# Stationary weight tiles stored in seven turns of layout in a two-block forward pass on one core

## The chip, the cores and the metric

The kernel runs on one core of a Trainium2 chip. The metric is the device time of one execution in microseconds (us), the median of the runs shown. The core has TensorE (PE in the profile, with its weight loads shown apart as PEld), VectorE (DVE), ScalarE (ACT), GpSimd (POOL) and the DMA queues, of which SP issues the weight loads.

## The reference, cut to what matters

Two blocks follow one another on 512 tokens of width 1024, float32 throughout. The first adds 16 meta tokens, and computes

```
n  = rms(h);  z = n @ w_in                     # q, k, v, glu, two gates: 7168 columns
u  = silu(layernorm(conv31(glu_a * sigmoid(glu_b)))) @ w_conv_out
m  = sigmoid(g_att) * diff_attention(q, k, v) + sigmoid(g_conv) * u
h  = h + m @ w_out
gate, val = split(conv3(rms(h) @ w_up))        # 2 x 2816 columns
h  = h + (silu(gate) * val) @ w_down
x  = rms(h)
```

The second block does this twice (two layers): `proj = rms(x) @ w_in` with 8192 columns, a gated three-tap convolution on one half, rotary retention with eight heads on the other half, then `x = x + rms(mix @ w_out)`.

Nearly all arithmetic is in these products with weights. Each is done in three TensorE passes: every operand is split into a high part of a short type (fp32r) and the remainder, and the product is high x high + low x high + high x low.

## The kernel before, in words

The activations lie with the model dimension on the partitions: eight tiles of 128 partitions by 512 to 528 token columns, once as the high part (`xh`) and once as the low part (`xl`), in one buffer `xhome`. A weight tile is 128 partitions by 1024 float32 columns (768 for the third part of w_down): eight 128x128 blocks beside one another, one for each 128 rows of the product's inner dimension.

`order` (line 75 on) lists the 300 weight tiles in the order in which they are used. `prep` (line 125) takes the next: SP's queue loads it into `wraw` (line 134, two buffers), ACT rounds it into `wh` (line 137), DVE subtracts to get `wl` (line 138). `getw` (line 141) keeps LOOK + 1 = 4 tiles prepared. 24 of the tiles hold the weights of v; in these products the weights are the moving operand (lines 473 and 806). The other 276 are stationary: `proj` (line 150) runs, for one output tile of n token columns in PSUM, three passes over the eight blocks, that is 24 matmuls at line 156 (18 for the short w_down tile), each with a 128x128 block of `wh` or `wl` as the stationary operand (its own weight load) and n columns of `xh` or `xl` as the moving one.

The column counts n follow the stage: 264 and 264 for the glu tiles (16 tiles, names gv and gg) and for k; 258 and 256 for q, the two gates (ga, gc), w_conv_out (yc) and w_out (wo); 258 and 258 for w_up (up, 44 tiles); 512 for w_down (dn), for the second block's projections (rq, rk, rz, cc, cx, cb, cz) and its w_out (w), except for the last tile of w_down, q and k of the first head of a layer and the last two outputs of a layer, which run as 256 and 256. By these loops line 156 issues 9522 matmuls: 5892 of 256 to 264 columns and 3630 of 512.

The program is written with a planner that orders each engine's instructions from its own estimate of durations; pools give the buffers, and a tile's writer waits for the readers of the buffer's last content. The 31-tap convolution of the first block runs on DVE (line 399) during the attention, at a low priority.

Of the kernel before, what the change touches and what calls it, by code (L numbers as in the profile page):

```python
# [14 lines left out]
ALU = mybir.AluOpType  # L15
# [3 lines left out]
P = 128  # L19
# [21 lines left out]
KB = 1  # L41
PSF = (4, 3, 1)
GC_EARLY = 5

PAR = {}
_off = 0
# [16 lines left out]
def kernel(ctx, tc, hT, par, pos, decay, w1, w2, out):  # L63
    nc = tc.nc
    V, S, PE = nc.vector, nc.scalar, nc.tensor
# [7 lines left out]
    def fv(ap):  # L73
        return ap.bitcast(F32)


    order = []

    def w1_tiles(name, idx):
        order.append((w1[name], idx))  # L80

    for cc in range(NK):
        w1_tiles("w_in", 24 + cc)
        w1_tiles("w_in", 32 + cc)
    for h in range(HEADS):
        if h % 2 == 0:
            order.append((w1["w_v"], h))
            order.append((w1["w_v"], h + 1))
        w1_tiles("w_in", h)
        w1_tiles("w_in", 8 + h)  # L90
        if h < HEADS - 1:
            w1_tiles("w_in", 40 + h)
        if h < GC_EARLY:
            w1_tiles("w_in", 48 + h)
    w1_tiles("w_in", 40 + HEADS - 1)
    for n in range(GC_EARLY, NK):
        w1_tiles("w_in", 48 + n)
# [6 lines left out]
        w1_tiles("w_up", NF + j)  # L104
    for n in range(NK):
        for g in range(3):
            order.append((w1["w_down"], (n, g, slice(None), slice(0, (8, 8, 6)[g] * P))))
    for l in range(2):
        for h in range(HEADS):
            if h % 2 == 0:  # L110
                order.append((w2["w_v"], (l, h)))
                order.append((w2["w_v"], (l, h + 1)))
            for base in (32, 40, 56):
                order.append((w2["w_in"], (l, base + h)))
        for cc in range(NK):
            for base in (8, 16, 0, 24):
                order.append((w2["w_in"], (l, base + cc)))
        for n in range(NK):
            for g in (1, 0):
                order.append((w2["w_out"], (l, n, g)))  # L120

    ready = []
    state = {"next": 0}

    def prep():
        if state["next"] >= len(order):
            return
        src, idx = order[state["next"]]
        i = state["next"]
        state["next"] += 1  # L130
        src = src[idx]
        n = src.shape[1]
        raw = wpool.tile([P, D], F32, tag="wraw", bufs=2, name=f"wraw{i}")[:, :n]
        nc.sync.dma_start(raw, src)
        wl = wpool.tile([P, D], F32R, tag="wl", name=f"wl{i}")
        wh = wpool.tile([P, D], F32R, tag="wh", name=f"wh{i}")
        S.copy(wh[:, :n], raw)  # L137
        V.tensor_tensor(wl[:, :n], raw, fv(wh[:, :n]), ALU.subtract)  # L138
        ready.append((wh, wl))

    def getw():
        while len(ready) < LOOK + 1 and state["next"] < len(order):
            prep()
        return ready.pop(0)

    def ks(k):
        return slice(k * P, (k + 1) * P)

    def proj(ps, w, xh, xl, t0, n, nk=NK, first=True, last=True, late=0):


        wh, wl = w
        passes = ((wh, xh), (wl, xh), (wh, xl))
        steps = [(a, b, k) for r in (range(nk - late), range(nk - late, nk)) for a, b in passes for k in r]
        for i, (a, b, k) in enumerate(steps):
            PE.matmul(ps, lhsT=a[:, ks(k)], rhs=b[k][:, t0:t0 + n],  # L156
                      start=first and i == 0, stop=last and i == len(steps) - 1)

    def split(src, hi, lo):
# [22 lines left out]
    def later(steps, by=20000):  # L182

        at_ = tc.cur_priority
        tc.cur_priority = at_ + by
        steps()
        tc.cur_priority = at_


    class SumSq:  # L190


        def __init__(self, tag, slot="nacc"):
            self.acc = npool.tile([P, T1], F32, tag=slot, name=f"acc_{tag}")
            self.tag, self.seen = tag, {}
# [45 lines left out]
    def mmA(name):  # L241
        return psA.tile([P, 512], F32, tag="mm", name=name)
# [15 lines left out]
    for c0, cn in C528:  # L258
        for j in range(NK // 2):
            nc.sync.dma_start(ht2[j][:, :, c0:c0 + cn], hT[2 * j:2 * j + 2, :, c0:c0 + cn].rearrange("k p t -> p k t"))  # L260
            if c0 == 0 and j in (0, 3):
                prep()
        if c0 == 0:
            nc.sync.dma_start(pr[:, 8:], par[:, 8:])

    xu = [[hpool.tile([P, T1], F32R, tag=f"x{p}", name=f"xu{p}{k}") for k in range(NK)] for p in "hl"]
    for c0, cn in C528:
        c = slice(c0, c0 + cn)
# [109 lines left out]
    for i, (q0, qn, nkey) in enumerate(QT):  # L378
        nb = -(-nkey // P)
        t = ap1.tile([P, nb * P], F32, name=f"a{i}")  # L380
# [51 lines left out]
    def g_conv(n):  # L432
        w = getw()
        if n < 6:
            t = ap1.tile([P, TQ], F32, name=f"tgc{n}")
        else:
            t = upool.tile([P, CONV_K - 1 + T1], F32, tag="u", name=f"tgc{n}")
        for i, (c0, cn) in enumerate(C514):
            ps = mmA(f"gc{n}_{i}")[:, :cn]
            proj(ps, w, xh, xl, TQ0 + c0, cn)  # L440
            S.activation(t[:, c0:c0 + cn], ps, AF.Tanh, scale=0.5)
        tgc.append(t)

    def g_att(h):
        w = getw()
        tg = ap2.tile([P, TQ], F32, tag="tga", name=f"tga{h}")
        for i, (c0, cn) in enumerate(C514):
            ps = mmA(f"ga{h}_{i}")[:, :cn]
            proj(ps, w, xh, xl, TQ0 + c0, cn)
            S.activation(tg[:, c0:c0 + cn], ps, AF.Tanh, scale=0.5)  # L450
        return tg
# [8 lines left out]
    for h in range(HEADS):  # L460
# [3 lines left out]
        if h % 2 == 0:  # L464
            wa, wb = getw(), getw()
            for tb in range(5):
                m = P if tb < 4 else META
                ps = mmA(f"v{h}_{tb}")[:m, :256]
# [9 lines left out]
        for i, (c0, cn) in enumerate(C514):  # L478
            ps = mmA(f"q{h}_{i}")[:, :cn]
            proj(ps, w, xh, xl, TQ0 + c0, cn)  # L480
            c = slice(c0, c0 + cn)
# [11 lines left out]
        for i, (c0, cn) in enumerate(C528):  # L493
            ps = mmA(f"k{h}_{i}")[:, :cn]
            proj(ps, w, xh, xl, c0, cn)
            c = slice(c0, c0 + cn)
# [5 lines left out]
        if h < HEADS - 1:  # L502
            tg = g_att(h)
        if h < GC_EARLY:
            g_conv(h)
        if h == HEADS - 1:
            att_rstd(("kf", "kl"))
            tg = g_att(h)
            later(norm_2, N2)
            for n in range(GC_EARLY, NK):  # L510
                later(lambda: g_conv(n), GCL)
# [11 lines left out]
        for t, (q0, qn, nkey) in enumerate(QT):  # L523
# [3 lines left out]
            if t < 4:  # L527
                ps = psS.tile([P, 2, 512], F32, tag="ps", name=f"s{h}_{t}")
# [9 lines left out]
            else:  # L538
                for m in range(2):
                    ps = psS.tile([P, 1024], F32, tag="ps", name=f"s{h}_{t}_{m}")  # L540
# [23 lines left out]
            src = ptr[:, :nb * qw].rearrange("p (b q) -> p b q", b=nb)  # L564
# [3 lines left out]
        for aT, q0, qn, blocks in (  # L568
# [10 lines left out]
            ps = psO.tile([P, 512], F32, tag="tr", name=f"pss{h}_{q0}")  # L579
            if h < HEADS - 1:  # L580
                PE.matmul(ps[:, :qn], lhsT=ones, rhs=sq[:, :qn], start=True, stop=True)
                g, r = SSQ[h]
# [12 lines left out]
    for n in range(NK):  # L595
        w = getw()
        for i, (c0, cn) in enumerate(C514):
            c = slice(c0, c0 + cn)
            ps = mmA(f"yc{n}_{i}")[:, :cn]
            proj(ps, w, uh, ul, c0, cn)  # L600
            V.scalar_tensor_tensor(tgc[n][:, c], tgc[n][:, c], 1.0, ps, ALU.add, ALU.mult)
        for i, (c0, cn) in enumerate(C514):
            c = slice(c0, c0 + cn)
            pb = rs7[:, c]
            if n < NK - 1:
                pb = mmA(f"rb{n}_{i}")[:, :cn]
                g, r = SSQ[n]
# [22 lines left out]
    for n in range(NK):  # L630
# [4 lines left out]
        t = lp2.tile([P, TQ], F32, tag="hre", name=f"hre{n}")  # L635
        nc.gpsimd.dma_start(t, hT[n][:, TQ0:])
        for i, (c0, cn) in enumerate(C514):
            ps = psM.tile([P, 512], F32, tag="mm", name=f"wo{n}_{i}")[:, :cn]
# [15 lines left out]
    def mmF(name):  # L654
        return psF.tile([P, 512], F32, tag="mm", name=name)
# [6 lines left out]
    for i, (c0, cn) in enumerate(C514):  # L662
        c = slice(c0, c0 + cn)
# [36 lines left out]
    for j in range(NF):  # L700
# [5 lines left out]
        for half in range(2):  # L706
            w = getw()
            f = half * NF + j
            for c in range(2):
                ps = mmF(f"up{f}_{c}")[:, :258]  # L710
                proj(ps, w, xh, xl, c * 256, 258)
                g = fp2.tile([P, 258], F32, tag="cg", name=f"cg{f}_{c}")
                V.tensor_tensor(g, ps, rs[:, c * 256:c * 256 + 258], ALU.mult)  # L713
                t = fp2.tile([P, 256], F32, tag=f"cv{half}", bufs=3 - half, name=f"cv{f}_{c}")
# [19 lines left out]
    for n in range(NK):  # L734
        ps = mmF(f"dn{n}")
        ws = [getw() for g in range(3)]
        for c0, cn in HALF if n == NK - 1 else ((0, SEQ),):
            c = slice(c0, c0 + cn)
# [4 lines left out]
        for c0, cn in HALF:  # L743
            c = slice(c0, c0 + cn)
# [10 lines left out]
    for l in range(2):  # L755
# [16 lines left out]
        else:  # L772
            for h0, hn in HALF:
                c = slice(h0, h0 + hn)
# [19 lines left out]
        for h in range(HEADS):  # L794
# [60 lines left out]
            ps = mmF(f"rz{l}{h}")  # L855
# [5 lines left out]
            for j, i0 in enumerate((0, 128, 256, 384)):  # L861
                n = SEQ - i0
                ps = psR.tile([P, 512], F32, tag="st", name=f"st{l}{h}{j}")[:, :n]
# [34 lines left out]
        for cc in range(NK):  # L898
            def ctile(tag, n=SEQ):

                if cc == 1 and tag == "yv":
                    return npool.tile([P, T1], F32, tag="nacc2", name=f"{tag}{l}{cc}")
                if cc == 1:
                    slot = {"pp": "csr", "ct": "snr"}[tag]
                    return b2pool.tile([P, 2 + SEQ], F32, tag=slot, name=f"{tag}{l}{cc}")
                if cc == 0:
                    return npool.tile([P, T1], F32, tag="ntmp", bufs=3, name=f"{tag}{l}{cc}")
                return cp.tile([P, n], F32, tag=tag, name=f"{tag}{l}{cc}")
# [3 lines left out]
            ps = mmF(f"cc{l}{cc}")  # L912
            proj(ps, getw(), xh, xl, 0, SEQ)
            t = ctile("ct")[:, :SEQ]
            V.tensor_tensor(t, ps, rs2, ALU.mult)
            ps = mmF(f"cx{l}{cc}")
# [7 lines left out]
            ps = mmF(f"cb{l}{cc}")  # L924
# [3 lines left out]
            ps = mmF(f"cz{l}{cc}")  # L928
# [137 lines left out]
```

## Time and profile before

| | |
|---|---|
| median of 2 runs | 1887.53 us (1887.47 to 1887.59) |
| the profiled execution's own time | 1886.62 us |
| its span on the core | 1884.7 us |
| mean granted TensorE clock | 0.995 of full speed |
| PE busy, weight loads busy | 98%, 89% of the span |
| DVE, ACT, POOL busy | 70%, 44%, 4% of the span |
| moved by DMA | 177.79 MB, mean 94 GB/s |

The span is the time from the first to the last instruction of the profiled execution; 1.9 us of its time lie around it. A matmul's busy time in the profile includes its way through the array, so matmuls that follow one another overlap in the record; what one costs in a row of many is read from the distance between their starts. The chain that ended last tells which engine's work set the time in each stretch.

### The profile page before, as it was taken

The page shows a single profiled execution, that of the slowest core. Times are in us where ns is not written, and L with a number is a line of the kernel's source. Part 1 is how long each engine was busy: PE and PEld are TensorE (multiplying, and loading weights), DVE is VectorE, ACT ScalarE, POOL GpSimd, SP SyncE. Part 2 cuts the span into 40 slices and gives each one's busy share as a digit, 9 for nine tenths or more (in the row PEclk, how much of TensorE's full clock was granted, in tenths as well). Part 3 has the DMA queues.
Part 4 walks back from the last instruction along what each step waited for, and adds up shares of the span by engine and source line. Part 5 has one row for each costly group of instructions (what it writes and reads, how often), then busy time and mean ns, then how long its engine had stood idle before and what let it go on. Part 6 is the DMA issues. An engine that isn't in the chain of part 4 may idle for free.

```text
span 1884.7 us, 29258 instructions
## 1 busy us (share of the span) xinstructions
PE 1854.0 (98%) x11802; PEld 1685.0 (89%) x11802; DVE 1312.0 (70%) x2147; ACT 838.6 (44%) x1475; POOL 75.9 (4%) x123
## 2 busy tenths in 40 slices
PE   8999999989999999999999999999999999999997
PEld 7999999989999999988988888888898888888887
DVE  8999999766788777634588776554277877745424
ACT  7234455584445445433356553222255555422222
POOL 3000011000000000000000000000020000000000
PEclk9999999999999999999999999999999999999999
DMA  4332323213332222232223232232223222233231
GB/s 153 101 113 91 102 83 110 91 57 101 107 101 96 96 91 90 86 102 94 100 79 101 79 98 92 90 101 97 93 68 101 95 96 89 78 101 99 91 101 56
DMA packets 53047, 177.79 MB, mean 94 GB/s; under 512 B 6640, under 2 KB 10736, under 8 KB 52912
## 3 DMA queue, kind: packets, MB, share of 16 engines
q1 hardware_dynamic: 47696, 160.80, 25.5%
q0 software_dynamic: 5072, 15.12, 3.0%
q8 instruction: 93, 1.52, 0.3%
q14 instruction: 42, 0.34, 0.1%
q10 hardware_dynamic: 144, 0.00, 0.0%
HBM read 165.25 MB, written 2.10 MB: 89 GB/s over the span
## 4 chain that ended last, share of the span: by engine, by line
PE 94%; ACT 2%; DVE 2%; issue 1%; POOL 0%; DMA 0%; DVEq 0%; ACTq 0%; POOLq 0%
PE up L156 13%; PE w L156 9%; PE dn L156 6%; PE rz L156 5%; PE cb L156 5%; PE cc L156 5%; PE cx L156 5%; PE cz L156 5%; PE rv L806 5%; PE rq L156 5%; PE rk L156 5%; PE v L473 3%; PE k L156 3%; PE wo L156 2%; PE q L156 2%; PE ga L156 2%
## 5 line engine op out<-in xcount | busy, mean ns | idle before, releaser
L137 ACT CAST wh<-wraw 128x1024 fp32r<-128x1024 f32 (+1 forms) x300 | 313.3, 1045 | 485.3 <-PE dn L156 66.8
L138 DVE TENSOR_TENSOR wl<-wraw,wh 128x1024 fp32r<-128x1024 f32 (+1 forms) x300 | 364.2, 1215 | 187.7 <-ACT wh L137 187.0
L156 PE MATMUL up<-xhome,wh 128*128 128x258 f32 x1408 | 184.0, 282 | 0.0
L156 PEld LDWEIGHTS up<-xhome,wh 128*128 128x128 f32 x1408 | 175.1, 188 | 0.1
L399 DVE SCALAR_TENSOR_TENSOR y<-u,pr,y 128x514 f32<-128x514 f32 x240 | 170.5, 742 | 0.4 <-ACT y L397 0.2
L156 PE MATMUL up<-xhome,wl 128*128 128x258 f32 x704 | 98.8, 282 | 0.0
L156 PEld LDWEIGHTS up<-xhome,wl 128*128 128x128 f32 x704 | 90.4, 188 | 0.0
L719 DVE SCALAR_TENSOR_TENSOR cv<-cg,pr,cv 128x256 f32<-128x256 f32 x176 | 83.7, 479 | 7.9 <-ACT cv L716 6.5
L716 ACT ACTIVATE cv<-cg,pr 128x256 f32<-128x256 f32 x88 | 52.6, 598 | 63.6 <-DVE cg L713 63.6
L806 PE MATMUL rv<-wh,xhome 128*128 128x256 f32 x512 | 75.4, 286 | 0.3 <-ACT xhome L232 0.3
L156 PE MATMUL rq<-xhome,wh 128*128 128x512 f32 (+1 forms) x288 | 69.9, 372 | 1.1 <-ACT xhome L232 1.0
L806 PEld LDWEIGHTS rv<-wh,xhome 128*128 128x128 f32 x512 | 67.8, 191 | 2.0 <-ACT xhome L232 0.6
L156 PE MATMUL rk<-xhome,wh 128*128 128x512 f32 (+1 forms) x288 | 68.6, 369 | 0.0
L156 PE MATMUL w<-ml,wh 128*128 128x512 f32 (+1 forms) x320 | 66.9, 350 | 0.0
L156 PE MATMUL w<-mh,wh 128*128 128x512 f32 (+1 forms) x320 | 66.6, 350 | 0.0
L156 PE MATMUL w<-mh,wl 128*128 128x512 f32 (+1 forms) x320 | 66.2, 349 | 0.0
L156 PE MATMUL rz<-xhome,wh 128*128 128x512 f32 x256 | 66.0, 392 | 0.0
L156 PE MATMUL cx<-xhome,wh 128*128 128x512 f32 x256 | 64.0, 390 | 0.0
L156 PE MATMUL cc<-xhome,wh 128*128 128x512 f32 x256 | 63.7, 390 | 0.0
L156 PE MATMUL cb<-xhome,wh 128*128 128x512 f32 x256 | 63.7, 390 | 0.0
L889 DVE RECIPROCAL rsq<-rsq 128x512 f32<-128x512 f32 x16 | 53.6, 3350 | 14.1 <-ACT rsq L888 14.1
L156 PE MATMUL cz<-xhome,wh 128*128 128x512 f32 x256 | 63.3, 389 | 0.0
(377 smaller groups left out, 3993.7 us busy)
## 6 DMA issues: line engine op xcount, KB each, us to landing
wraw<-w_in SPq DMA_DIRECT2D x160, 512.0 KB, 3.2
wraw<-w_up SPq DMA_DIRECT2D x44, 512.0 KB, 3.2
wraw<-w_out SPq DMA_DIRECT2D x40, 512.0 KB, 3.2
wraw<-w_v SPq DMA_DIRECT2D x24, 512.0 KB, 3.2
wraw<-w_down SPq DMA_DIRECT2D x16, 512.0 KB, 3.2
qh<-qf POOLq DMA_DIRECT2D x32, 129.0 KB, 2.7
wraw<-w_conv_out SPq DMA_DIRECT2D x8, 512.0 KB, 3.2
dc<-dec POOLq DMA_DIRECT2D x16, 256.0 KB, 3.0
```

The costliest lines, as they stand in the source:

```text
L137: S.copy(wh[:, :n], raw)
L138: V.tensor_tensor(wl[:, :n], raw, fv(wh[:, :n]), ALU.subtract)
L156: PE.matmul(ps, lhsT=a[:, ks(k)], rhs=b[k][:, t0:t0 + n], start=first and i == 0, stop=last and i == len(steps) - 1)
L399: V.scalar_tensor_tensor(ys[i][:, :TQ], src, wj, ys[i][:, :TQ], ALU.mult, ALU.add)
L473: PE.matmul(ps, lhsT=x, rhs=w, start=p == 0 and k == 0, stop=p == 2 and k == NK - 1)
L716: S.activation(t, g[:, 0:256], AF.Identity, scale=pr[:, o:o + 1], bias=pc("ffn_dw_b", f))
L719: V.scalar_tensor_tensor(t, g[:, k:k + 256], pr[:, o:o + 1], t, ALU.mult, ALU.add)
L806: PE.matmul(ps, lhsT=xx, rhs=w, start=p == 0 and k == 0, stop=p == 2 and k == NK - 1)
L889: V.reciprocal(rr, rr)
```

## The change

Each stationary tile gets one of seven layouts by its turn in the order (276 tiles, the turn counted modulo 7): plain; two, four or eight parts interleaved column by column in `wh` and `wl` (kind W); or plain storage, with the moving columns and the PSUM columns walked in pieces of 8, 16 or 32, taken in turn from the first and the second half of the range (kind M). The v tiles stay as they were.

For kind W with s parts, the tile's n columns are cut into s equal parts, and column m of part j is stored at position m*s + j. ACT and DVE read `wraw` in order and write with a step of s elements (DVE also reads `wh` with that step); a weight load of one 128x128 block then reads 128 columns that lie s elements (4s bytes) apart. A 768-column tile takes 2 parts where 4 or 8 do not divide its six blocks. For kind M the stored tile and the weight load are as before, and `move` reorders the moving columns and the PSUM columns in the same way; where n is not a multiple of 256 (264 and 258), it leaves both as they were. The number of instructions, the DMAs and the arithmetic are the same.

```diff
+WEAVE = (('W', 1), ('W', 2), ('W', 4), ('W', 8), ('M', 8), ('M', 16), ('M', 32))
...
-        order.append((w1[name], idx))
+        order.append((w1[name], idx, True))
...
-            order.append((w1["w_v"], h))
+            order.append((w1["w_v"], h, False))
...
+    class Woven:
+        def __init__(self, t, n, kind, c):
+            self.t, self.n, self.kind = t, n, kind
+            self.s = (c if n // P % c == 0 else 2) if kind == "W" else 1
+            self.c = c if kind == "M" else 0
+
+        def parts(self):
+            if self.s == 1:
+                return self.t[:, :self.n]
+            return self.t[:, :self.n].rearrange("p (m s) -> p s m", s=self.s)
+
+        def plain(self, ap):
+            return ap.rearrange("p (s m) -> p s m", s=self.s) if self.s > 1 else ap
+
+        def block(self, k):
+            if self.s == 1:
+                return self.t[:, k * P:(k + 1) * P]
+            j = self.n // P // self.s
+            return self.parts()[:, k // j, k % j * P:(k % j + 1) * P]
+
+        def move(self, ap):
+            n = ap.shape[-1]
+            if not self.c or n % 256:
+                return ap
+            return ap.rearrange("p (two m c) -> p m two c", two=2, c=self.c)
...
-        S.copy(wh[:, :n], raw)
-        V.tensor_tensor(wl[:, :n], raw, fv(wh[:, :n]), ALU.subtract)
-        ready.append((wh, wl))
+        c = ("W", 1)
+        if stationary:
+            c = WEAVE[state["woven"] % len(WEAVE)]
+            state["woven"] += 1
+        th, tl = Woven(wh, n, *c), Woven(wl, n, *c)
+        S.copy(th.parts(), th.plain(raw))
+        V.tensor_tensor(tl.parts(), th.plain(raw), fv(th.parts()), ALU.subtract)
+        ready.append((th, tl) if stationary else (wh, wl))
...
-            PE.matmul(ps, lhsT=a[:, ks(k)], rhs=b[k][:, t0:t0 + n],
+            PE.matmul(a.move(ps), lhsT=a.block(k), rhs=a.move(b[k][:, t0:t0 + n]),
                       start=first and i == 0, stop=last and i == len(steps) - 1)
```

## Rows read from the trace of the kernel before

**Rows 1.** The page, busy time: share of the span, instructions.

```profile
span 1884.7 us, 29258 instructions
...
PE 1854.0 (98%) x11802; PEld 1685.0 (89%) x11802; DVE 1312.0 (70%) x2147; ACT 838.6 (44%) x1475; POOL 75.9 (4%) x123
```

**Rows 2.** The page, the chain that ended last, shares by engine and by line.

```profile
PE 94%; ACT 2%; DVE 2%; issue 1%; POOL 0%; DMA 0%; DVEq 0%; ACTq 0%; POOLq 0%
PE up L156 13%; PE w L156 9%; PE dn L156 6%; PE rz L156 5%; PE cb L156 5%; PE cc L156 5%; PE cx L156 5%; PE cz L156 5%; PE rv L806 5%; PE rq L156 5%; PE rk L156 5%; PE v L473 3%; PE k L156 3%; PE wo L156 2%; PE q L156 2%; PE ga L156 2%
```

**Rows 3.** The chain in order of time: start, length, engine, tile, matmuls.

```profile
49.53 2.90 PE gv L156 x24
...
539.72 247.09 PE up L156 x2059
...
1145.77 5.44 PE cc L156 x24
```

**Rows 4.** Busy time by stretch: length; PE, PEld, DVE, ACT, POOL; clock, DMA.

```profile
0.00:108.00 108.00, 98.85 (x774) 97.18 (x774) 99.44 (x173) 50.60 (x92) 17.14 (x20) 1.00 0.36 121
108.00:240.00 132.00, 131.02 (x1076) 128.13 (x1076) 125.66 (x244) 58.38 (x142) 12.46 (x24) 1.00 0.33 101
240.00:380.00 140.00, 140.00 (x1143) 136.57 (x1142) 125.85 (x241) 81.47 (x201) 16.34 (x32) 1.00 0.33 99
...
533.00:787.00 254.00, 254.00 (x2116) 253.91 (x2115) 205.26 (x414) 126.53 (x225) 0.00 (x0) 1.00 0.28 92
...
1118.00:1298.00 180.00, 180.00 (x804) 149.32 (x803) 101.27 (x127) 56.28 (x69) 0.00 (x0) 1.00 0.28 94
```

**Rows 5.** What TensorE waited for: us in total, times, longest.

```profile
PE gv L156 <- ACT wh L137: 6.3, 1, 6.3
...
PE gg L156 <- DVE wl L138: 0.6, 1, 0.6
```

**Rows 6.** Weight loads by shape: count, busy us, mean ns, idle before.

```profile
L156 PEld LDWEIGHTS up<-xhome,wh 128*128 128x128 f32 x1408 | 175.1, 188 | 0.1
...
L563 PEld LDWEIGHTS tr<-ident,a 128*128 128x128 f32 x72 | 8.4, 140 | 1.4 <-ACT aTA L566 1.2
L473 PEld LDWEIGHTS v<-wh,xhome 128*16 128x16 f32 x64 | 6.0, 94 | 1.3
```

**Rows 7.** Weight loads in time, 118 to 123 us: start, length, tile, count.

```profile
120.34 0.89 PEld L473 LDWEIGHTS v<-wl,xhome 128*16 128x16 f32 x8
121.25 0.89 PEld L473 LDWEIGHTS v<-wh,xhome 128*16 128x16 f32 x8
```

**Rows 8.** Weight loads in time at 1011 us, around matmuls of 128 columns.

```profile
1011.40 0.19 PEld L865 LDWEIGHTS st<-qh,kh 128*128 128x128 f32 x1
1011.52 0.19 PEld L865 LDWEIGHTS st<-qh,kl 128*128 128x128 f32 x1
1011.63 0.19 PEld L865 LDWEIGHTS st<-ql,kh 128*128 128x128 f32 x1
1011.74 0.19 PEld L876 LDWEIGHTS ro<-sh,rvh 128*128 128x128 f32 x1
1011.85 0.19 PEld L876 LDWEIGHTS ro<-sh,rvl 128*128 128x128 f32 x1
```

**Rows 9.** The copies into the weight tiles, by shape: count, busy us, mean ns.

```profile
L137 ACT CAST wh<-wraw 128x1024 fp32r<-128x1024 f32 x292 | 306.6, 1051 | 453.5 <-PE cx L156 66.6 <-issue 65.1 <-PE cz L156 64.6
```

**Rows 10.** The same on DVE.

```profile
L138 DVE TENSOR_TENSOR wl<-wraw,wh 128x1024 fp32r<-128x1024 f32 x292 | 356.5, 1222 | 159.2 <-ACT wh L137 158.6
```

More of the change, by code (lines that the diff above doesn't have):

```diff
@@ L86 @@
         if h % 2 == 0:
-            order.append((w1["w_v"], h))
-            order.append((w1["w_v"], h + 1))
+            order.append((w1["w_v"], h, False))
+            order.append((w1["w_v"], h + 1, False))
         w1_tiles("w_in", h)
@@ L106 @@
         for g in range(3):
-            order.append((w1["w_down"], (n, g, slice(None), slice(0, (8, 8, 6)[g] * P))))
+            order.append((w1["w_down"], (n, g, slice(None), slice(0, (8, 8, 6)[g] * P)), True))
     for l in range(2):
@@ L110 @@
             if h % 2 == 0:
-                order.append((w2["w_v"], (l, h)))
-                order.append((w2["w_v"], (l, h + 1)))
+                order.append((w2["w_v"], (l, h), False))
+                order.append((w2["w_v"], (l, h + 1), False))
             for base in (32, 40, 56):
-                order.append((w2["w_in"], (l, base + h)))
+                order.append((w2["w_in"], (l, base + h), True))
         for cc in range(NK):
             for base in (8, 16, 0, 24):
-                order.append((w2["w_in"], (l, base + cc)))
+                order.append((w2["w_in"], (l, base + cc), True))
         for n in range(NK):
             for g in (1, 0):
-                order.append((w2["w_out"], (l, n, g)))
+                order.append((w2["w_out"], (l, n, g), True))
     ready = []
-    state = {"next": 0}
+    state = {"next": 0, "woven": 0}
+    class Woven:
[19 more added lines that the diff above has]
+            return ap.rearrange("p (two m c) -> p m two c", two=2, c=self.c)
     def prep():
@@ L127, in prep @@
             return
-        src, idx = order[state["next"]]
+        src, idx, stationary = order[state["next"]]
         i = state["next"]
```

## The prediction, made before the change was run

> **What bounds the kernel now.** I read the busy shares first, then the chain that ended last, then the same chain in order of time, then the busy time by stretch, and last the weight loads one by one. TensorE is busy for 1854.0 of 1884.7 us [rows 1], and the chain gives it 94% of the span, nearly all of it at line 156, the line that the change rewrites [rows 2]. So the time is the number of matmul steps times the distance between their starts, plus some 31 us in which TensorE is idle. A change that touches neither the number nor the distance can win no more than a part of these 31 us, and the change removes no wait; that is why I give a gain of over 2% (38 us) next to nothing.
>
> The distance is what the change can move, and the chain in time gives it for both widths [rows 3]: 2059 steps of 258 columns in 247.09 us are 120.0 ns each, and 24 steps of 512 in 5.44 us are 226.7 ns. The 254 additional columns cost 106.7 ns, 0.42 ns a column (2.4 GHz; the granted clock is 1.00 in these stretches [rows 4]); 258 x 0.42 is 108 ns, so some 12 ns of a short step are not streaming.
>
> How close is the weight load to setting the distance? Load records overlap, so their lengths hold a fixed part: 188 ns for 128 columns against 94 ns for 16 [rows 6], that is 0.84 ns a column and some 81 ns fixed. 128 columns are thus 107.5 ns of loading, about the streaming of a short step. Two places confirm it. Around matmuls of 128 columns (54 ns of streaming) loads start 110 to 120 ns apart, four steps in 0.45 us, 113 ns [rows 8]: that is the distance the load alone forces, 107.5 + 5.5. With stationary operands of 16 columns, eight steps of 256 columns take 0.91 us, 114 ns [rows 7], against 120 with a full load. So a short step has almost no cover for a slower load: anything beyond 113 ns soon shows. A 512-column step covers a load of about 220 ns. In the stretch of w_up the load row is busy for 253.91 of 254.00 us; in the second block's convolution, with 512 columns, for 149.32 of 180.00 [rows 4].
>
> **The change part by part.** I counted the layouts by walking the order of the 276 tiles. Of the short steps (256 to 264 columns) 864 get two parts, 864 four, 768 eight; of the 512-column steps 558, 504 and 528. The M kinds reorder 756 steps of 256 and 1542 of 512; in 258 and 264 columns they do nothing, and w_up has no reordered step at all.
>
> *Weight loads with a step.* The trace has no load whose columns lie apart, so I bound it. A load cannot become faster: the lower end is 0. For the upper end: the fastest reading by TensorE that the rows show is the moving one, 4 bytes in 0.42 ns, which is 16 bytes in 1.68 ns. If TensorE reads 16 bytes at a time and no faster than that, a load with columns 16 or 32 bytes apart pays 1.68 ns a column, 215 ns in place of 107.5; with columns 8 bytes apart it gets two from each reading, 0.84 ns, and pays nothing. The load alone would then force 113 + 107.5 = 220.5 ns: a short step goes from 120 to 220.5 (+100.5), a 512-column step stays at 226.7. The upper end is (864 + 768) x 100.5 ns = 164 us. I take 0, by the transposes: they load 128 columns of float32 in 140 ns, 48 ns less than line 156 does [rows 6], so an ordinary load of the same bytes is not held at 188 by the reading; the reading can be slower by some 0.37 ns a column before it shows. That leans to the lower end; it does not exclude the upper one, so both stay for the range.
>
> The Trainium skill speaks against this: SBUF — State Buffer, Specifications (TRN2), has 16-byte lines that need at least two hits each for full bandwidth, every crossing to a new line paying a penalty. By that rule the four- and eight-part loads would be penalised and the two-part ones not; it gives no size, and no row here shows it. The sum by it would be the upper end above, if the penalty is one more reading time.
>
> *Moving and PSUM columns in pieces.* All reading is of runs of 32 bytes or more, so no more 16-byte readings arise than before (where the run starts aligned). What is open is a cost at each change of half. The pieces are 522 x 64 + 240 x 32 for pieces of 8, 522 x 32 + 204 x 16 for 16, and 498 x 16 + 312 x 8 for 32: 71,520 in all. Lower end 0. Upper end: each piece costs what a whole new instruction costs beyond its columns, 114 - 107.5 = 6.5 ns [rows 7], 465 us. [...] I take 0; one lost column time per piece would be 71,520 x 0.42 ns = 30 us.
>
> *The copies into the tiles.* 119 tiles are written with a step (42, 39 and 38). ACT's copy is 1051 ns [rows 9] and DVE's 1222 ns [rows 10]; both go at about one element a nanosecond. Lower end 0, upper end twice: 1.05 us and 1.22 us a tile. ACT has the room (81.47 of 140.00 us in its fullest stretch shown [rows 4]). DVE has 31 us free up to 380 us (99.44, 125.66 and 125.85 busy of 108, 132 and 140 [rows 4]), and about 20 of the 119 tiles fall there: 24 us in the upper case, still inside. The cover is also the three tiles kept ahead, over 15 us of TensorE work; only the first tiles lack it (6.3 us and 0.6 us of waiting [rows 5]), where two slow copies would add some 2 us. If DVE's free time in that stretch were gone, its low-priority convolution would end later, and the steps of w_conv_out behind it would wait. I take 0 for the copies.
>
> *What does not move.* The DMAs, their queue and the instructions are the same in number. The planner may order a few instructions otherwise; that plays on the 31 us idle, and I give it plus or minus 5 us.
>
> The sum is 1886.6 (the profiled execution, 1884.7 span and 1.9 around it) + 0 + 0 + 0, which is 0.9 below the median of the runs. With a little for the first copies: **1888 us**.
>
> **The rivals.** *A slower load at four and eight parts* (the other side): place, the 1632 short steps of line 156, half of them in w_up, k and glu; price 100.5 ns each; 1886.6 + 164 = 2051 us, or 2062 if the 12 ns of a step are kept beyond the longer load (107.5 each). It decides from the point where a load exceeds the 113 ns that the rows show. For it: the load row without a gap in w_up [rows 4]. Against it: the faster transpose load [rows 6]. Chance 0.22.
>
> *Only eight parts are slower*: if a reading brings 32 bytes in place of 16, a four-part load still gets two columns from each and an eight-part load one: 768 x 100.5 ns = 77 us, 1964 us. For and against as above; the unit is in no row. The same Trainium skill page (Door 1: The DMA port swizzle) has a sentence by which a step of 4 fp32 is free; no run here shows which of the two holds. Chance of this rival 0.08.
>
> *Pieces cost in the moving walk*: 30 us at one column time, 1917 us, just within 2%; more if a turn costs more. For it: 64 pieces in a step are many; against: nothing in the rows, none walks in pieces. Chance 0.08, half of it beyond 2%.
>
> *Slow writes by DVE and ACT that show* in the first 430 us: up to the 24 us of DVE above, 1911 us. For it: DVE at 92% there [rows 4]; against: TensorE rarely waits for a copy [rows 5]. Chance 0.05.
>
> *The change does less than it says*: for M in 258 and 264 columns it does nothing, as counted; that is already in the sums and has no chance of its own.
>
> **How the numbers follow.** 2% is about what a measurement of this kernel tells from no change. The forecast has 0.55, its own range 1882 to 1900. Within 2%: 0.55 + half of the pieces 0.04 + most of the writes 0.04 = 0.63. Slower: 0.22 + 0.08 + 0.04 + 0.01 = 0.35. Faster: 0.02, for a planner's order that I cannot see. Leaving out the load case would leave more than 2 in 10 outside, so the range goes from 1880 (a better order) to 2063, the load case at its dearer end; outside are larger penalties and dear pieces, some 6 in 100.
>
> **What would show it.** Right: the chain of w_up still at 120 ns a step, all seven layouts alike, loads at 188 ns. The load rival: load records of four- and eight-part tiles some 107 ns longer (near 295 ns), runs of 24 steps in w_up at about 5.3 us between runs at 2.9, and the 512-column steps unchanged. The pieces: 512-column steps longer than 5.44 us for 24 in three tiles of seven, most in pieces of 8. The writes: lines 137 and 138 with longer maxima and TensorE waits on them. A two-part load that is slower too, or a load penalty above one reading time (512-column steps growing as well), would make the prediction wrong on the far side.

## The result, and the profile after

The changed kernel takes 2121.03 us (median of 2 runs, 2120.76 to 2121.30) against 1887.53: a ratio of 1.1237 (95% interval 1.1189 to 1.1285), 233.5 us more. The forecast was 1888; the rival on the slower side was 2051 to 2062, and the range ended at 2063. So the direction came from the rival, and even the rival was 59 us short.

The page of the changed kernel, to be held against [rows 1], has TensorE busier by the whole difference (2086.7 - 1854.0 = 232.7 us), the weight loads, whose records overlap, by 259 us, and DVE and ACT by 67 and 81 us:

```profile
span 2119.2 us, 29260 instructions
...
PE 2086.7 (98%) x11802; PEld 1944.0 (92%) x11802; DVE 1379.3 (65%) x2147; ACT 919.9 (43%) x1475; POOL 77.6 (4%) x123
```

The number of matmuls is the same, so it is the distance between starts that grew. The chain in order of time, to be held against [rows 3] (start, length, engine, tile, matmuls), shows it for both widths; the seven rows of the second block follow one another in the order of the seven layouts, plain first:

```profile
650.99 319.90 PE up L192 x2059
...
1393.20 5.49 PE cc L192 x24
1398.68 5.60 PE cx L192 x24
1404.29 5.64 PE cb L192 x24
1409.93 5.89 PE cz L192 x24
1415.82 5.84 PE cc L192 x24
1421.66 5.76 PE cx L192 x24
1427.42 5.68 PE cb L192 x24
```

In w_up a step went from 120.0 to 155.4 ns on average. In the 512-column steps every layout costs something: 5.49 us for 24 steps in place of 5.44 for plain tiles, then 5.60, 5.64 and 5.89 for two, four and eight parts, and 5.84, 5.76 and 5.68 for pieces of 8, 16 and 32.

Inside w_up the weight loads in order of time separate the layouts, because a chain's eight loads of `wl` stand as a row of their own; from its start to the start of the next row are eight steps:

```profile
719.91 2.03 PEld L192 LDWEIGHTS up<-xhome,wl 128*128 128x128 f32 x8
721.84 2.98 PEld L192 LDWEIGHTS up<-xhome,wh 128*128 128x128 f32 x16
...
727.64 1.03 PEld L192 LDWEIGHTS up<-xhome,wl 128*128 128x128 f32 x8
728.60 1.99 PEld L192 LDWEIGHTS up<-xhome,wh 128*128 128x128 f32 x16
...
754.53 1.96 PEld L192 LDWEIGHTS up<-xhome,wl 128*128 128x128 f32 x8
756.40 3.83 PEld L192 LDWEIGHTS up<-xhome,wh 128*128 128x128 f32 x16
```

The first pair is an eight-part tile, 1.93 us or 241 ns a step; the second a tile whose turn is pieces of 8 (without effect in 258 columns), 0.96 us or 120 ns; the third a four-part tile, 1.87 us or 234 ns. Two-part tiles stand at 122 ns in the same view.

The distances between starts, times the counts of the prediction, give the bill:

| layout | step of 256 to 264 columns | step of 512 | cost, us |
|---|---|---|---|
| plain | 120 | 229 (+2) x 498 | 1 |
| two parts | 122 (+1.7) x 864 | 233 (+7) x 558 | 5 |
| four parts | 233 (+113) x 864 | 235 (+8) x 504 | 102 |
| eight parts | 241 (+121) x 768 | 246 (+19) x 528 | 103 |
| pieces of 8 | 122 to 182 | 243 (+17) x 522 | 12 |
| pieces of 16 | 120 to 150 | 240 (+13) x 522 | 8 |
| pieces of 32 | 120 to 134 | 237 (+10) x 498 | 6 |

The sum is 237 us against 233.5 measured. The surplus lies in the w_out stage of the second block, where plain steps of 512 columns took some 232 ns before the change already (the bill takes 226.7 as their base).

### The profile page after: what moved, and what is told of

The parts are those of the page before. It is cut to its first block, busy times and chain, and to the rows that moved or that the text cites. A ratio compares the mean times of both kernels' runs of the same rounds, so it can differ in the third digit from the quotient of the medians.

```text
span 2119.2 us, 29260 instructions
## 1 busy us (share of the span) xinstructions
PE 2086.7 (98%) x11802; PEld 1944.0 (92%) x11802; DVE 1379.3 (65%) x2147; ACT 919.9 (43%) x1475; POOL 77.6 (4%) x123
## 4 chain that ended last, share of the span: by engine, by line
PE 93%; DVE 3%; ACT 2%; issue 1%; DMA 0%; POOL 0%; DVEq 0%; ACTq 0%; POOLq 0%
PE up L192 15%; PE w L192 8%; PE dn L192 6%; PE rz L192 4%; PE cc L192 4%; PE cx L192 4%; PE cb L192 4%; PE cz L192 4%; PE rk L192 4%; PE rq L192 4%; PE rv L842 4%; PE ga L192 3%; PE gc L192 3%; PE gv L192 3%; PE v L509 3%; PE gg L192 3%
## 5 line engine op out<-in xcount | busy, mean ns | idle before, releaser
L173 ACT CAST wh<-wraw 128x1024 fp32r<-128x1024 f32 (+1 forms) x300 | 400.0, 1336 | 505.7 <-PE dn L192 69.9
L174 DVE TENSOR_TENSOR wl<-wraw,wh 128x1024 fp32r<-128x1024 f32 (+1 forms) x300 | 435.0, 1451 | 255.2 <-ACT wh L173 254.7
L192 PE MATMUL up<-xhome,wh 128*128 128x258 f32 x1408 | 232.9, 317 | 0.0
L192 PEld LDWEIGHTS up<-xhome,wh 128*128 128x128 f32 x1408 | 225.1, 233 | 0.1
L192 PE MATMUL up<-xhome,wl 128*128 128x258 f32 x704 | 123.3, 317 | 0.0
L192 PEld LDWEIGHTS up<-xhome,wl 128*128 128x128 f32 x704 | 115.8, 233 | 0.0
L749 DVE TENSOR_TENSOR cg<-up,rs_ffn 128x258 f32<-128x258 f32 x88 | 37.2, 423 | 65.1 <-PE up L192 64.7
L192 PE MATMUL rk<-xhome,wh 128*128 128x512 f32 (+1 forms) x288 | 74.5, 390 | 0.0
L192 PEld LDWEIGHTS rk<-xhome,wh 128*128 128x128 f32 x288 | 59.2, 234 | 7.5 <-issue 0.5
```

The source lines that it names most:

```text
L173: S.copy(th.parts(), th.plain(raw))
L174: V.tensor_tensor(tl.parts(), th.plain(raw), fv(th.parts()), ALU.subtract)
L192: PE.matmul(a.move(ps), lhsT=a.block(k), rhs=a.move(b[k][:, t0:t0 + n]), start=first and i == 0, stop=last and i == len(steps) - 1)
```

## The experiments

Theory after the result: TensorE reads its memory in 16-byte units, and a weight load pays for every unit that it touches; 512 columns of streaming hide such a load, 258 do not. Rivals: the cost sits in the copies or the planner's order; the pieces and the interleaved tiles cost one another; a distance of 16 bytes is a cliff.

**The distance alone.** Edit: plain storage, and a load that takes columns 1 to 8 elements apart, in eight turns.

```diff
-WEAVE = (('W', 1), ('W', 2), ('W', 4), ('W', 8), ('M', 8), ('M', 16), ('M', 32))
+WEAVE = tuple(('W', s) for s in range(1, 9))
...
-            j = self.n // P // self.s
-            return self.parts()[:, k // j, k % j * P:(k % j + 1) * P]
+            a = min(k * P, self.n - P * self.s)
+            return self.t[:, a:a + P * self.s].rearrange("p (m s) -> p s m", s=self.s)[:, 0, :]
```

> The tiles are stored plainly, no columns walk in pieces; eight turns only change which columns a weight load reads: 128 columns that lie 1, 2, ... 8 elements apart inside the tile (so the blocks are not the right ones: the arithmetic is changed, the number of instructions is not). It gives the price of a short step (258 columns) against the distance. Theory A, TensorE reads 16 bytes at a time, 1.68 ns each, and a load pays for every 16-byte unit that it touches: distances 1 and 2 about 120 and 122 ns a step, 3 (96 units) about 175, 4 to 8 (128 units) 233 to 241; whole time near 2380 us. Theory B, a cliff: any distance below 16 bytes is free, so 3 stays near 122; near 2340 us. Theory C, 8-byte units: 3 is already at 233; near 2425 us. The 8 ns by which eight parts were dearer than four: if units lie in two alternating banks, only distance 8 (always the same bank) shows 241, and 5, 6 and 7 stay near 233.

Measured: 2344.94 us (one run). The same view as above, in w_up, for distances 3, 4, 5 and 8, two rows each:

```profile
854.89 1.47 PEld L190 LDWEIGHTS up<-xhome,wl 128*128 128x128 f32 x8
856.28 3.34 PEld L190 LDWEIGHTS up<-xhome,wh 128*128 128x128 f32 x16
...
865.12 1.96 PEld L190 LDWEIGHTS up<-xhome,wl 128*128 128x128 f32 x8
866.99 3.77 PEld L190 LDWEIGHTS up<-xhome,wh 128*128 128x128 f32 x16
...
876.09 1.90 PEld L190 LDWEIGHTS up<-xhome,wl 128*128 128x128 f32 x8
877.90 3.72 PEld L190 LDWEIGHTS up<-xhome,wh 128*128 128x128 f32 x16
...
909.55 2.03 PEld L190 LDWEIGHTS up<-xhome,wl 128*128 128x128 f32 x8
911.49 2.98 PEld L190 LDWEIGHTS up<-xhome,wh 128*128 128x128 f32 x16
```

The starts are 1.39 us apart for distance 3 (174 ns a step), 1.87 for 4 (234), 1.81 for 5 (226) and 1.94 for 8 (242); distance 2 stands at 122, 6 at 227 and 7 at 234. Distance 3 decides: 174 is what 96 units were to cost (175), neither 122 (a cliff at 16 bytes) nor 233 (units of 8 bytes). From 4 on each column has a unit of its own. The whole time fell on the cliff's number by chance: the eight turns do not have equal shares of the short steps, and the measured prices times the true counts give some 2358 us (an estimate), 13 more than measured. The two-bank idea for the dearer eighth distance fails: 7 is dearer than 5 and 6 as well.

**The copies alone.** Edit: storage in parts as in the change, every load from neighbouring columns, no pieces.

```diff
+WEAVE = (('W', 1), ('W', 2), ('W', 4), ('W', 8), ('W', 1), ('W', 1), ('W', 1))
...
         def block(self, k):
...
+            return self.t[:, k * P:(k + 1) * P]
```

> The tiles are stored in 1, 2, 4 or 8 parts as in the change, but every weight load reads 128 neighbouring columns and nothing walks in pieces (the blocks are then not the right ones: the arithmetic is changed). It shows alone what the stepped writes and reads of ACT and DVE and the planner's order cost. Theory, the cost is in TensorE's loads and pieces: 1885 to 1895 us, with the copies of four- and eight-part tiles longer but covered. Rival, the copies are late for TensorE in the first 430 us: 1900 to 1920 us.

Measured: 1895.88 us, a ratio of 1.0039 (1.0024 to 1.0054), 7.8 us more, just above the theory's span. The groups of the copies by shape, to be held against [rows 9, 10]:

```profile
L171 DVE TENSOR_TENSOR wl<-wraw,wh 128x1024 fp32r<-128x1024 f32 x292 | 426.7, 1463 | 184.9 <-ACT wh L170 184.1
L170 ACT CAST wh<-wraw 128x1024 fp32r<-128x1024 f32 x292 | 391.4, 1344 | 379.3 <-PE cx L189 60.6 <-PE cz L189 60.3 <-issue 51.9
```

Split by turn, ACT's copy takes 1052 ns plain, 1127 with two parts, 2035 with four and 2207 with eight; DVE's 1224, 1226, 2033 and 2250 (medians of the 1024-column tiles). So the stepped copy does cost double, 70 us of DVE and 85 of ACT, and about nine tenths of that is hidden. How much of the 7.8 us is left in the change, where TensorE takes longer, no run shows: the bill above comes out without it. What shows is at the beginning, where no tile is ahead (TensorE waits 9.7 us for ACT's copies in place of 6.3), and in the first 540 us: w_up's first full stretch starts at 547.38 in place of 539.72 and lasts 247.09 us as before.

**Only the interleaved turns, only the pieces.** Edits: the other turns plain.

```diff
+WEAVE = (('W', 1), ('W', 2), ('W', 4), ('W', 8), ('W', 1), ('W', 1), ('W', 1))   # first
+WEAVE = (('W', 1), ('W', 1), ('W', 1), ('W', 1), ('M', 8), ('M', 16), ('M', 32)) # second
```

> The interleaved layouts in their turns as in the change, plain walks in the place of the three M kinds. By the distances between matmul starts in the two traces, four parts cost 101 us, eight parts 97, two parts 3 and the M kinds 28 of the 232 that they add up to. If the parts add: 2093 us (2121 less 28). If the pieces also delay the neighbouring tiles: below 2085.

> Only the three M kinds in their turns, the other four turns plain. By the distances between starts the M kinds cost 28 us: 1915 us if the parts add. A rival, that the M price was a consequence of slow neighbours: 1888 to 1895 us.

Measured: 2097.01 us (ratio 1.1106, 1.1089 to 1.1122) and 1911.79 us (1.0125, 1.0108 to 1.0142). The additions to the kernel before on the same chip (1888.05) are 209.0 and 23.7 us, together 232.7 of the 233.5: the parts add, neither causes the other.

**The length of a piece.** Edit: no interleaved tiles, pieces of 2 to 64.

```diff
+WEAVE = (('W', 1), ('M', 2), ('M', 4), ('M', 8), ('M', 16), ('M', 32), ('M', 64))
```

> No interleaved tiles; the turns are plain and pieces of 2, 4, 8, 16, 32 and 64 columns (the computation is the reference's). Theory, TensorE reads the moving operand in 16-byte units at no more than one in 1.68 ns: a 512-column step is 227 ns plain, about 233 to 243 for pieces of 64 to 8, 245 to 250 for pieces of 4 (still one unit per four columns), and with pieces of 2 every unit brings only two of its four columns, 256 units, 430 ns and 13 around it: about 443. Whole time near 2050 us. Rival, a price per change of half (0.26 ns by the pieces of 8): 2 would be 227 + 67 = 294, 4 about 260; near 1960 us.

Measured: 1991.43 us, between the two. The chain in order of time, plain and then pieces of 2, 4, 8 and 16 (24 steps of 512 columns each):

```profile
1192.80 5.44 PE cx L192 x24
1198.23 8.15 PE cb L192 x24
1206.39 6.00 PE cz L192 x24
1212.39 5.84 PE cc L192 x24
1218.23 5.76 PE cx L192 x24
```

Pieces of 2 cost 340 ns a step, not 443: a unit of which two columns are used takes about 1.3 ns (an estimate, (340 - 13) / 256), less than the 1.68 that I had taken as the least. Nor is it a price per change of half: pieces of 64, 32, 16, 8, 4 and 2 (8 to 256 pieces) add 2, 10, 13, 17, 23 and 113 ns. Both theories missed.

**Which side of the walk.** Edit: only the moving columns (R) or only the PSUM columns (O) in pieces.

```diff
+WEAVE = (('W', 1), ('R', 8), ('O', 8), ('M', 8), ('R', 32), ('O', 32), ('M', 32))
...
+            PE.matmul(a.move(to) if a.kind != "R" else to, lhsT=a.block(k), rhs=a.move(of) if a.kind != "O" else of,
```

> The seven turns: plain; moving columns alone in pieces of 8; PSUM columns alone in pieces of 8; both; the same three with 32 (where only one side walks in pieces, the columns of the product come out in another order: the arithmetic is changed). Theory, the price lies in reading: moving alone costs what both cost (512 columns: 243 ns with 8, 237 with 32; about 180 for 256 columns that start 8 bytes off a 16-byte unit), PSUM alone stays at 227. Rival, it lies in the writes to PSUM: the other way round.

The same view, plain, then moving alone, PSUM alone and both, in pieces of 8:

```profile
1169.58 5.44 PE cx L193 x24
1175.02 5.84 PE cb L193 x24
1180.86 5.45 PE cz L193 x24
1186.31 5.84 PE cc L193 x24
```

The price is the moving operand's, all of it; writing PSUM in pieces is free here. With pieces of 32 the three rows are 5.67, 5.46 and 5.68 us.

**Where a run starts.** Edit, in the kernel with the pieces alone:

```diff
-C514 = ((0, 258), (258, 256))
+C514 = ((0, 256), (256, 258))
```

> As the run with the pieces alone, but the 514 columns of the first block are cut as 256 + 258 in place of 258 + 256. The 256-column part of w_conv_out and w_out then starts at a multiple of 16 bytes, that of q and the gates 8 bytes past one. Theory, a piece that starts inside a unit touches one unit more, 1.7 to 1.8 ns a piece: w_conv_out and w_out in pieces of 8 fall from about 180 to 122 to 127 ns a step, and q and the gates rise from about 125 to 180. Rival, it belongs to these stages and not to where the run starts: unchanged. The whole time says little: 1912 to 1917 us.

Weight loads of w_out in pieces of 8, 256 columns, six steps from row to row, first with the cut as in the change (the run with the pieces alone), then swapped, with the gate's rows ahead:

```profile
516.89 1.09 PEld L192 LDWEIGHTS wo<-mh,wl 128*128 128x128 f32 x6
517.97 1.11 PEld L192 LDWEIGHTS wo<-ml,wh 128*128 128x128 f32 x6
```

```profile
135.29 1.42 PEld L192 LDWEIGHTS ga<-xhome,wl 128*128 128x128 f32 x8
136.69 2.49 PEld L192 LDWEIGHTS ga<-xhome,wh 128*128 128x128 f32 x16
...
523.40 0.78 PEld L192 LDWEIGHTS wo<-mh,wl 128*128 128x128 f32 x6
524.12 0.78 PEld L192 LDWEIGHTS wo<-ml,wh 128*128 128x128 f32 x6
```

w_out falls from 180 to 120 ns a step, and the gate, now starting 8 bytes past a unit, goes to 175 (1.40 us for eight). The price moved with the start: 58 ns for 32 pieces, 1.8 ns for the one further unit of each. With 16 and 32 columns it is 1.7 to 1.9 a piece. The whole time was 1917.07 us.

**The load alone.** Edit, in the kernel with the distances: 64 columns streamed.

```diff
-            PE.matmul(a.move(ps), lhsT=a.block(k), rhs=a.move(b[k][:, t0:t0 + n]),
+            m = n if i == 0 or (last and i == len(steps) - 1) else 64
+            PE.matmul(ps[:, :m], lhsT=a.block(k), rhs=b[k][:, t0:t0 + m],
```

> As the run with distances 1 to 8, but all matmuls of line 156 other than a chain's first (and the last one of a finished sum) stream 64 columns in place of 256 to 512, so that the distance between starts is the load's alone (the arithmetic is changed). Theory, a load takes the larger of 0.84 ns a column and 1.68 ns a 16-byte unit, and 5.5 ns: distances 1 and 2 113 ns, 3 near 167, 4 to 8 all near 220; what 233 and 241 hold beyond 220 with 258 columns then comes from the load and the moving operand in each other's way. Rival, the distance itself makes a load dearer: 4, 7 and 8 stay above 5 and 6 here too, at 226 to 241. The whole time is of no use, other engines set it in part: 1300 to 1700 us.

Measured: 2588.0 us, far above the 1300 to 1700 expected. TensorE streamed little between its loads, and its mean granted clock was 0.595: 2.4 GHz in some stretches, 1.2 in most. That gave the test a second clock. The busy time of two stretches (the granted clock is the third number from the end):

```profile
682.50:685.50 3.00, 2.73 (x26) 2.62 (x24) 3.00 (x6) 2.95 (x6) 0.00 (x0) 1.00 0.00 0
1042.00:1060.00 18.00, 18.00 (x84) 18.00 (x84) 9.05 (x17) 4.95 (x9) 0.00 (x0) 0.50 0.09 30
```

and the loads in order of time: distance 8 and distance 1 (plain) at 2.4 GHz, then the same two at 1.2 GHz:

```profile
673.51 2.00 PEld L191 LDWEIGHTS gc<-xhome,wl 128*128 128x128 f32 x8
675.42 1.98 PEld L191 LDWEIGHTS gc<-xhome,wh 128*128 128x128 f32 x8
...
682.42 0.98 PEld L191 LDWEIGHTS yc<-xhome,wh 128*128 128x128 f32 x8
683.32 0.97 PEld L191 LDWEIGHTS yc<-xhome,wl 128*128 128x128 f32 x8
...
1042.24 2.00 PEld L191 LDWEIGHTS up<-xhome,wl 128*128 128x128 f32 x8
1044.15 3.71 PEld L191 LDWEIGHTS up<-xhome,wh 128*128 128x128 f32 x16
...
1047.74 1.83 PEld L191 LDWEIGHTS up<-xhome,wl 128*128 128x128 f32 x8
1049.45 3.54 PEld L191 LDWEIGHTS up<-xhome,wh 128*128 128x128 f32 x16
```

A plain load forces 112 ns at 2.4 GHz and 214 at 1.2; a load at distance 8 forces 239 at both. Distances 4, 5, 6 and 7 alone give 233, 223, 223 and 231 at both clocks, and 3 gives 173 and 213. So from 16 bytes on the load's time does not follow the array's clock, which fits a load that waits for the memory, and the differences among the distances are the load's own: the theory that they come from the moving operand fell, the rival stands. Why 5 and 6 are cheaper than 4 and 8 stays open.

**Cover.** Edit, in the change:

```diff
             c = WEAVE[state["woven"] % len(WEAVE)]
+            if c in (("W", 4), ("W", 8)) and i in SHORT:    # tiles used with 256 to 264 columns
+                c = ("W", 2)
```

> The change, but tiles that are used with 256 to 264 columns and whose turn is four or eight parts get two; tiles used with 512 columns keep all seven layouts (the computation is the reference's). Theory, a load of 220 ns is hidden under 512 columns and bare under 258: of the 233 us, the 184 that the distances between starts give to four and eight parts in short steps go, two parts cost 3 in their place: 1932 to 1942 us. Rival, much of the price is elsewhere (copies, order): above 1960.

Measured: 1934.20 us, a ratio of 1.0247 (1.0230 to 1.0264), as the theory had it. w_up's stretch is back at

```profile
547.36 248.62 PE up L195 x2059
```

120.8 ns a step with two-part tiles among them. The 187 us between this kernel and the change's 2121 hang on whether a slow load has 512 columns above it.

**Pieces with a small load.** Edit, in the kernel with the lengths: 16 stationary columns.

```diff
+            r = P if i == 0 or (last and i == len(steps) - 1) else 16
+            PE.matmul(a.move(ps[:r]), lhsT=a.block(k)[:, :r], rhs=a.move(b[k][:, t0:t0 + n]),
```

> As the run with pieces of 2 to 64 columns, but the loads take 16 columns in place of 128 (all but the first of a chain and the last of a finished sum; the arithmetic is changed, the streaming is not). It shows whether the 10 to 16 ns that pieces of 32 to 8 cost a 512-column step are the moving operand's own. Theory, they come from load and moving operand reading the same memory out of step: plain falls from 227 to about 220, and pieces of 8, 16 and 32 to 220 too. Rival, every change of half costs: 233 to 236 for pieces of 8, 230 to 233 for 16 and 32. Pieces of 2 stay above 300 in both.

Chain in order of time, pieces of 2, pieces of 8, plain (1979.75 us in all):

```profile
1190.43 7.87 PE cb L193 x24
...
1204.23 5.84 PE cc L193 x24
...
1227.06 5.50 PE cc L193 x24
```

Pieces of 8 cost 243 ns as with the full load, and plain did not fall (229); pieces of 2 fell from 340 to 328. The price of pieces of 8 is in the moving operand's reading, not in a collision with the load; the theory fell, and the rival, which had 233 to 236 for them, had the size too low.

**The place of a tile.** Edit: plain tiles in buffers 32 bytes longer, stored from 0 to 8 columns past their start.

```diff
+            at = WEAVE[state["woven"] % len(WEAVE)]      # 0, 1, 2, 3, 4, 6, 8
+            wh, wl = wh[:, at:], wl[:, at:]
```

> All tiles plain and no pieces, but the tiles are stored (and loaded) from 0, 1, 2, 3, 4, 6 or 8 columns past the buffer's start, in turns (the computation is the reference's). A load of 128 neighbouring columns that starts inside a 16-byte unit touches 33 units in place of 32. Theory, a unit more or less is nothing against the 107 ns of shifting: 120 and 227 ns at every offset, 1886 to 1892 us. Rival, a collision of the load's and the moving operand's units makes the 6 ns by which a short step is above 114: then some offset shows 114 and the time falls below 1884 us.

Measured: 1904.30 us, 17.8 more, which neither theory had. In the chain no offset stands apart: 24 steps of the convolution take 5.49 to 5.64 us, here with offsets of 0 and 1:

```profile
1160.42 5.59 PE cx L193 x24
1166.01 5.61 PE cb L193 x24
```

against 5.44 before, while a step of w_up rose by 0.6 ns. The w_out of the second block, 576 of the 3630 steps, did not rise; its row before the change and here:

```profile
1298.09 78.33 PE w L156 x384
...
1310.74 78.13 PE w L193 x384
```

So 3054 steps at 5 ns, 15 us, are most of the 17.8. The buffers' new length moved every tile, the offset 0 among them. In the program of the kernel before, those 3054 steps have a load and a moving row that both start at multiples of 256 bytes, and take 227 ns; the 576 of w_out have a moving row 128 or 192 bytes past one, and took 232 to 233 already. Inside this run, 126 of the steps whose distance the trace gives still have both starts at multiples of 256 bytes, and they take 227.7 ns on average; 2754 whose moving row alone starts there take 232.5 (some of their load starts, 240 bytes past a multiple, take 227.5 too). So the places of the two operands carry this cost, but no run varied them alone, and the rule behind them stays open.

## Why the prediction was wrong

- **What bounds the kernel**: right. The time is the number of steps times their distance, 120.0 and 226.7 ns were the right base (232 in the second block's w_out), and a short step had no cover: a load beyond 113 ns showed at once.
- **The step that failed**: "Weight loads with a step ... I take 0, by the transposes." The runs showed 113 ns a step for four parts and 121 for eight. The transposes load *neighbouring* columns, four to a 16-byte unit; at 140 ns, less the 81 that are fixed, they take 0.46 ns a column, close to the moving operand's 0.42, which is what the 1.68 ns bound is made of. They say nothing about one column to a unit, so the row was no evidence against the upper end. Of the two rows, the one that measured the same quantity, units in a time, was the moving stream's. The Trainium skill's rule (SBUF — State Buffer, Specifications (TRN2): 16-byte lines, at least two hits) had four and eight parts dear and two free, and the loads of the short steps agree: +1.7 ns for two parts, +113 and +121 for the others. The sentence of the same Trainium skill page (Door 1: The DMA port swizzle) by which 4 fp32 is a free step does not agree: distance 4 costs 113 ns.
- **The upper end** was also too low: it had 100.5 ns, since it took every unit at 1.68 ns; the load alone shows up to 1.82 ((239 - 5.5) / 128), and 13 to 21 ns a step were missing, 26 us in all.
- **512-column steps "stay"**: roughly. A load of 220 to 240 ns is hidden but for 8 to 19 ns, 14 us for four and eight parts, and two parts cost 7.
- **Pieces, taken at 0**: 23.7 us by the run with them alone, near the 30 of the rival but by another rule. No run shows the 0 for the reading side: pieces of 32 to 8 added 10 to 17 ns to a 512-column step. The aside on aligned starts was right and worth 5 us. PSUM was free: the Trainium skill (PSUM — Partial Sum Buffer, Specifications (TRN2)) has any non-contiguous pattern slow matmuls significantly, which pieces of 8 and 32 there did not do (5.45 and 5.46 us against 5.44).
- **Copies, taken at 0**: double in duration as the upper end had it, 7.8 us in the time by the run with them alone. Cover held for the rest. (The 31 us of free DVE are 29 by the rows named: 380 less 350.95.)
- **Chances and range**: the load rival had 0.22 and was priced alone. Every unknown was bounded, but the range added none of the others' bounds to it; the load's true price in short steps (15 us above the dearer load case), the pieces (24) and the loads in long steps (some 19) lie 58 us above its end.

## What to carry to other kernels

Where the load row is busy without a gap and the streaming of a step is no longer than the load, price anything that slows a load at its full upper end. A row is evidence on a bound only if it measures the same quantity: an operation on neighbouring elements says nothing about spread ones. For operands of this width, keep stationary columns at most 8 bytes apart (8 bytes cost 2 ns a short step and 7 a long one, 12 bytes 54 a short one), start the pieces of a moving walk at multiples of 16 bytes, and if a layout must be spread, give it to tiles that stream 512 columns.

## What the runs showed of the hardware that was not expected

- A load with columns 16 or more bytes apart does not follow the array's clock: 239 ns at 2.4 and at 1.2 GHz for distance 8.
- Distances 5 and 6 (226 ns a short step) are cheaper than 4 and 7 (233) and 8 (241).
- 32 bytes more per weight buffer cost 17.8 us, some 5 ns on each of the 3054 steps of 512 columns outside w_out, with no instruction changed in shape or number.
